# Attention on a 4 by 64 grid: keys kept column by column, 416 of 512 keys per query tile

## The chip, the cores and the metric

The kernel runs on one NeuronCore of a Trainium2 chip. The core has a matrix engine (TensorE, PE in the profile, with its weight loads listed as PEld), three engines that work on rows of data (VectorE or DVE, ScalarE or ACT, GpSimd or POOL), a queue engine that mostly starts transfers (SyncE or SP), and DMA engines that move data between DRAM and the on-chip memory SBUF. Results of TensorE land in eight PSUM banks. Each engine works through its own list of instructions in order, and waits on semaphores where it needs another engine's result. The metric is the device time of one execution in microseconds, as a median over runs.

## What is computed

Two layers over 256 latent tokens (a grid of 4 rows and 64 columns, width 2048) and 256 context tokens. The first layer has 16 heads of neighbourhood attention beside a state-space mixer (SSD, 8 groups of 4 heads); their outputs, gated, go through one output projection. The second is a short gated convolution. The change touches only the attention of the first layer:

```
rows = seq // GRID_W                       # 4; kh = min(8, rows) = 4, so every row sees all rows
col_start = clip(col - 8, 0, 48)           # a query column sees 16 key columns
mask      = (col' >= col_start) & (col' < col_start + 16)
s_lat = q . k * scale + rpb[h, row' - row + 7, clip(col' - col, -15, 15) + 15], masked to -inf
s_ctx = q . k_ctx * scale                  # all 256 context tokens, no bias
pr    = softmax([s_lat, s_ctx])            # 512 keys
out   = pr[:256] . v + pr[256:] . v_ctx
```

So each query has 4 x 16 latent keys and 256 context keys that count. Which latent keys these are depends on the query's column alone, not on its row. A block of queries of neighbouring columns needs only the keys of neighbouring columns.

## The kernel before

TensorE does nearly everything in three products: each float32 operand is split into a rounded part (type float32r) and the remainder, and H.H + H.L + L.H are added up in PSUM. `mm` (L195) issues every product, `turn` (L199) every transpose. Weights arrive from DRAM in tiles of 128 x 1024 (`raw`), are split by ACT (L420, rounded part) and DVE (L427, remainder) into one of three places `w`, and are used once.

The program works through one long sequence of weight products: the first 8 blocks of K, V, Q and B; then the gate, the time steps and the SSD inputs of the first quarter; then, for each further quarter, Q and K (`do_qk`), gate and V (`do_gv`), SSD inputs (`do_ssd`), with gate and V last in the last quarter; then the output projection in passes of 512 columns (the first pass does two of them), then the second layer. All other work is written as generators (`kq_gen`, `head_gen`, `group_gen`, `put_mix` and others) that hang between the weight products. A planner (class `Plan`) keeps a clock for each engine and prices each instruction as it is recorded. `pump` lets a generator go on when the planner's clocks say that its operands will be ready; `force`, called where the main sequence needs a result that is not recorded yet, records the pending steps in the order that the planner finds earliest, until that result is there. The order on each engine thus follows from the planner's prices: a change of one instruction can move many others. [...]

For one attention head (`head_gen`, L1033) the steps are: four transfers bring the head's bias rows from a staged copy in DRAM (`rpbs`, written at L929) into `bias` (L1039); DVE adds the column mask, 512 columns (L1044); for each of two query tiles of 128 queries (two grid rows), TensorE makes the scores against all 512 keys, 256 latent and 256 context (`score`, three products); DVE adds the bias and takes the row maximum (`top`, L1057), where the 256 context columns use a block of zeros that POOL has set (L932); ACT takes the exponential and its sum (L1062); DVE scales. TensorE transposes the weights in blocks of 128 keys, ACT and DVE split them into `PH` and `PL` (L1099, L1101), and V of the head into `VH` and `VL` (L1110, L1112). Then come 12 products: four key blocks, three products each, over all 256 queries. DVE multiplies with the gate (L1122), and `put_mix` (L939) writes the head's output to DRAM (L951) or, late in the program, splits it in place into a `mix` tile (L944, L946). K and Q of four heads at a time are normalised, transposed and split by `kq_gen` (L994, L996, L998, L1000); V goes from PSUM to `Vt` by `v_gen` (L1012).

An SSD group ends like this (`group_gen`, L1370): transfers bring decay rows from DRAM (L1391), ACT and DVE make the four decay matrices (the last product at L1420), TensorE multiplies them with the inputs `xtm`, DVE adds `yi` and gates with `sz` (L1439, L1442), ACT squares (L1444), DVE adds (L1449), TensorE sums over the channels against a column of ones, DVE and POOL make the inverse root (L1460, L1462), TensorE spreads it by two transposes of `r`, DVE scales (L1472), and `put_mix` hands two more `mix` tiles to the output projection. The output projection takes the 32 `mix` tiles in a fixed order: 0 to 11, 16 to 31, 12 to 15. Heads 12 to 15 are the last group of attention, 30 and 31 the last SSD group.

## Time and profile before

| | |
|---|---|
| median of three runs | 1762.85 us (1761.52 to 1763.02) |
| profiled execution | 1760.31 us, span 1758.5 us |
| mean granted TensorE clock | 0.999 |
| busy: PE, PEld, DVE, ACT, POOL | 1736.7, 1463.1, 1223.6, 773.4, 31.6 us |
| moved by DMA | 377.66 MB |
| DMA packets | 202536, of which 32384 under 512 B |

How to read the rows: a group has the line of the program, the engine, the operation, `written<-read` by the program's names, the shape and the count; after the bar its busy time and the mean length of one in ns; after the second bar the idle time of the engine just ahead of it and what ended it. A row of the timeline or the chain has its start and its length in us from the start of the span. Lengths of products include the pipeline's latency, so products overlap in the list, and the pace of a stream is read from the distance of the starts. A plain float32 product appears as two records.

### The profile page before, as it was taken

Reading aid. Unit: us, or ns where it says so; the run is one execution under the profiler, and the core shown is the slowest. Engines: PE = TensorE matmul, PEld = TensorE weight load, DVE = VectorE, ACT = ScalarE, POOL = GpSimd, SP = SyncE. Lnnn points to the kernel's source line nnn. Section 1 sums busy time; section 2 is a strip of 40 time slices with the busy share of each in tenths; the row PEclk is TensorE's granted clock in tenths of the full one; section 3 lists DMA queues with packets and bytes.
Section 4 is the critical chain, followed back from the end, with each engine's and each line's share of the span. In section 5 each row is a group of like instructions: output and inputs, shape, how many; then the busy total and the mean of one; then the engine's idle time right before and its main releaser. Section 6 shows DMA issues by size and latency. Waiting matters only on the chain.

```text
span 1758.5 us, 25025 instructions
## 1 busy us (share of the span) xinstructions
PE 1736.7 (99%) x9451; PEld 1463.1 (83%) x9451; DVE 1223.6 (70%) x1978; ACT 773.4 (44%) x1330; POOL 31.6 (2%) x28
## 2 busy tenths in 40 slices
PE   6999999999999999999999999999999999999998
PEld 4777988889888889888888898888888888888887
DVE  5666887878685878686877787787668555555554
ACT  5333544445242436343435343564446444444442
POOL 0000100001000000000000000000000000000000
PEclk9999999999999999999999999999999999999999
DMA  9987644686756767656776557768767666666563
GB/s 362 342 307 258 209 143 138 183 246 191 234 165 195 219 205 227 210 175 210 220 213 193 166 185 255 246 221 284 274 222 228 195 188 192 192 191 188 190 208 121
DMA packets 202536, 377.66 MB, mean 215 GB/s; under 512 B 32384, under 2 KB 69040, under 8 KB 202416
## 3 DMA queue, kind: packets, MB, share of 16 engines
q1 hardware_dynamic: 195152, 369.49, 65.5%
q10 hardware_dynamic: 7264, 6.58, 1.1%
q8 instruction: 74, 1.21, 0.3%
q14 instruction: 46, 0.38, 0.1%
HBM read 370.62 MB, written 6.71 MB: 215 GB/s over the span
## 4 chain that ended last, share of the span: by engine, by line
PE 94%; DMA 2%; DVE 2%; issue 1%; ACT 0%; POOL 0%; SPq 0%; ACTq 0%; DVEq 0%; POOLq 0%
PE bank L195 91%; PE bank L199 3%; DMA tmp<-dram_csr 1%; DVE w L427 1%; DMA raw<-in_ada 0%; DMA tmp<-dram_exr 0%; DMA raw<-in_adaT 0%; DVE tmp L1235 0%; ACT w L420 0%; POOL statk L572 0%; DVE mix L1562 0%; SPq L583 0%; DVE raw L823 0%; DVE tmp L603 0%; DVE Vt L1012 0%
## 5 line engine op out<-in xcount | busy, mean ns | idle before, releaser
L420 ACT CAST w<-raw 128x1024 fp32r<-128x1024 f32 x343 | 359.5, 1049 | 530.4 <-PE bank L195 447.7
L427 DVE TENSOR_TENSOR w<-raw,w 128x1024 fp32r<-128x1024 f32 x343 | 416.6, 1217 | 231.4 <-ACT w L420 230.1
L195 PE MATMUL bank<-hH,w 128*128 128x256 f32 (+1 forms) x2064 | 488.0, 324 | 1.2 <-DVE w L427 1.1
L195 PE MATMUL bank<-w,hH 128*128 128x512 f32 x1280 | 407.4, 396 | 2.7 <-ACT hH L757 2.5
L195 PEld LDWEIGHTS bank<-hH,w 128*128 128x128 f32 x2064 | 344.7, 188 | 34.2 <-DVE w L427 2.1
L195 PE MATMUL bank<-hL,w 128*128 128x256 f32 (+1 forms) x1040 | 334.3, 321 | 0.0
L195 PEld LDWEIGHTS bank<-w,hH 128*128 128x128 f32 x1280 | 237.7, 189 | 54.4 <-issue 4.0
L195 PE MATMUL bank<-w,hL 128*128 128x512 f32 x640 | 249.9, 391 | 0.1
L195 PEld LDWEIGHTS bank<-hL,w 128*128 128x128 f32 x1040 | 196.3, 189 | 14.9
L195 PE MATMUL bank<-w,h 128*128 128x512 f32 x768 | 179.7, 390 | 0.0
L823 DVE CUSTOM_DVE_ANT_0 raw<-raw,csb 128x1024 f32<-128x1024 f32 x128 | 155.4, 1219 | 26.2 <-DMA raw<-in_adaT 24.0
L195 PEld LDWEIGHTS bank<-w,h 128*128 128x128 f32 x768 | 143.6, 188 | 29.6
L195 PEld LDWEIGHTS bank<-w,hL 128*128 128x128 f32 x640 | 120.5, 188 | 25.4 <-DVE hL L763 0.6
L195 PE MATMUL bank<-w,mix 128*128 128x512 f32 x588 | 138.3, 391 | 0.9 <-DVE w L427 0.9
L195 PEld LDWEIGHTS bank<-w,mix 128*128 128x128 f32 x588 | 109.5, 188 | 24.0 <-DVE w L427 1.3
L1235 DVE SCALAR_TENSOR_TENSOR tmp<-bank,cwh,tmp 128x508 f32<-128x508 f32 (+1 forms) x96 | 71.0, 744 | 1.8
L195 PE MATMUL bank<-KL,h 128*128 128x512 f32 x264 | 63.8, 389 | 0.0
L427 DVE TENSOR_TENSOR KL<-raw,KL 128x1024 fp32r<-128x1024 f32 x32 | 39.1, 1223 | 33.1 <-ACT KL L420 33.1
L427 DVE TENSOR_TENSOR wL<-raw,wH 128x1024 fp32r<-128x1024 f32 x31 | 37.9, 1224 | 33.5 <-ACT wH L420 33.4
L427 DVE TENSOR_TENSOR QL<-raw,QT 128x1024 fp32r<-128x1024 f32 x32 | 39.2, 1224 | 29.8 <-ACT QT L420 29.8
L195 PEld LDWEIGHTS bank<-KL,h 128*128 128x128 f32 x264 | 49.5, 188 | 10.2
L195 PE MATMUL bank<-QT,h 128*128 128x512 f32 x168 | 56.2, 391 | 0.0
(291 smaller groups left out, 1984.7 us busy)
## 6 DMA issues: line engine op xcount, KB each, us to landing
raw<-in_w_in SPq DMA_DIRECT2D x196, 512.0 KB, 3.9
raw<-in_adaT SPq DMA_DIRECT2D x128, 512.0 KB, 4.8
raw<-in_sc_in SPq DMA_DIRECT2D x128, 512.0 KB, 3.8
raw<-in_w_out SPq DMA_DIRECT2D x64, 512.0 KB, 5.0
raw<-in_ada SPq DMA_DIRECT2D x34, 512.0 KB, 6.9
raw<-in_sc_out SPq DMA_DIRECT2D x32, 512.0 KB, 4.1
PT<-in_ada SPq DMA_DIRECT2D x16, 512.0 KB, 6.9
raw<-in_w SPq DMA_DIRECT2D x16, 512.0 KB, 6.1
```

The source lines that it names most:

```text
L195: E(T.matmul(o, l, r, start=start, stop=stop, skip_group_check=True))
L199: E(T.transpose(o, i, ident if k == 128 else ident[:k, :k]))
L420: E(S.copy(H, v))
L427: E(V.tensor_tensor(out=Lo, in0=v, in1=H.bitcast(F32), op=ALU.subtract))
L823: E(V.tensor_tensor_reduce(out=raw, in0=raw, in1=csb, scale=1.0, scalar=0.0, op0=ALU.mult, op1=ALU.add, accum_out=gp[:, h, m:m + 1]))
L1235: E(V.scalar_tensor_tensor(out=do, in0=di, scalar=cwh[:, 32 * k + ch:32 * k + ch + 1], in1=do, op0=ALU.mult, op1=ALU.add))
```

## The change

Latent keys, queries and values are put in column order (column first, the four rows inside it), and each query tile is now a block of 32 grid columns rather than two grid rows. Query tile 0 holds columns 0 to 31 and needs key columns 0 to 39, tile 1 holds columns 32 to 63 and needs key columns 24 to 63: 160 of the 256 latent keys. The 512 keys stand in the order key columns 0 to 31, context, key columns 32 to 63, so each tile's keys are one run of 416: positions 0 to 415 for tile 0, 96 to 511 for tile 1.

- Scores, bias, maximum, exponential and scaling take 416 columns. DVE clears the 96 columns left (`top`).
- The products with the values take the two context blocks for all 256 queries, and each of the two latent blocks (32 key columns) for the 160 queries that see it (`BLOCKS`).
- The bias comes as a table made on the host, 672 columns a head, in one transfer; the staged copy and POOL's zeros go. The mask is added in three pieces.
- K and Q are written in column order by strided writes; K's latent tiles and all of Q's remainders take two instructions each (`kq_gen`).
- V is put in column order by a way through DRAM: four transfers out on ACT's queue and one in on SP's, for each group of four heads (`turn_v`).
- The gate multiplication reads PSUM with a stride to bring the output back to row order.

```diff
+    vd = drt([256, 512], "vd")
-    rpbs = drt([16, 64, 320], "rpbs")
-    E(DMA.dma_start(rpbs, bass.AP(tensor=rpb.tensor, offset=76, ap=[[465, 16], [0, 64], [1, 320]])))
-    for b_ in bias:
-        E(G.memset(b_[:, 2, :], 0.0))
...
+    def columns(ap, t):
+        return ap.rearrange("p h (c r) -> p h r c", r=4)[:, :, 2 * t:2 * t + 2, :]
+
+    def turn_v(a):
+        for t in range(2):
+            for r in range(2):
+                yield W_("AQ", Vt[:, t, :])
+                E(DMA2.dma_start(vd.rearrange("(c r) n -> c r n", r=4)[:, 2 * t + r, :], Vt[64 * r:64 * r + 64, t, :]))
+        yield W_("SP", vd)
+        E(DMA.dma_start(Vt[:, 0:2, :], vd.rearrange("(t p) n -> p t n", p=128)))
+        got.add(("V", a))
...
# kq_gen, K (t < 2: latent)
-                E(S.copy(dst[:, :, o], four(pt)))
-                E(V.tensor_tensor(out=low[:, :, o], in0=four(pt), in1=dst[:, :, o].bitcast(F32), op=ALU.subtract))
+                for dh_, _, i in places_:
+                    E(S.copy(dh_, i))
+                yield W_("DVE", dst)
+                for dh_, dl_, i in places_:
+                    E(V.tensor_tensor(out=dl_, in0=i, in1=dh_.bitcast(F32), op=ALU.subtract))
...
# v_gen
-        got.add(("V", a))
+        yield from turn_v(a)
...
# head_gen
+    BLOCKS = ((1, 2, slice(0, 256)), (2, 3, slice(0, 256)), (0, 0, slice(0, 160)), (3, 1, slice(96, 256)))
-        for r in range(4):
-            E(DMA.dma_start(bt[64 * (r % 2):64 * (r % 2) + 64, r // 2, :].rearrange("p (a b) -> p a b", a=4),
...
+        E(DMA.dma_start(bf, rpb[hd]))
-        E(V.tensor_tensor(out=bv, in0=bv, in1=mask.unsqueeze(1).to_broadcast([128, 8, 64]), op=ALU.add))
+        for o_, m_ in ((0, mask[:, 0:32]), (304, mid), (544, mask[:, 32:64])):
+            n_ = m_.shape[-1]
+            bv = bf[:, o_:o_ + 4 * n_].rearrange("p (c r) -> p c r", r=4)
+            E(V.tensor_tensor(out=bv, in0=bv, in1=m_.unsqueeze(2).to_broadcast([128, n_, 4]), op=ALU.add))
+        span = lambda qt: slice(96 * qt, 96 * qt + 416)
-            mm(ps, QT[:, h, o], KT[:, h, :], True, False)
+            mm(ps[:, :416], QT[:, h, o], KT[:, h, k_], True, False)
...
+            E(V.memset(sp[:, 0:96] if qt else sp[:, 416:512], 0.0))
-            E(S.activation(sp, sp, AF.Exp, bias=s4[:, 2 + qt:3 + qt], scale=1.0, accum_out=s4[:, 4 + qt:5 + qt]))
+            E(S.activation(sc, sc, AF.Exp, bias=s4[:, 2 + qt:3 + qt], scale=1.0, accum_out=s4[:, 4 + qt:5 + qt]))
...
-        for kt in range(4):
-            mm(po[:, :256], VH[:, kt], PH[:, kt, :], kt == 0, False)
-            mm(po[:, :256], VH[:, kt], PL[:, kt, :], False, False)
-            mm(po[:, :256], VL[:, kt], PH[:, kt, :], False, kt == 3)
+        for i, (kt, vt, q_) in enumerate(BLOCKS):
+            mm(po[:, q_], VH[:, vt], PH[:, kt, q_], i == 0, False)
+            mm(po[:, q_], VH[:, vt], PL[:, kt, q_], False, False)
+            mm(po[:, q_], VL[:, vt], PH[:, kt, q_], False, i == 3)
...
+    spawn(urgent, turn_v(0))
     spawn(urgent, kq_gen("K", 0, parK, 4, statk, KT, KL, False), 4)
```

## The prediction

> **What bounds the kernel now.** I read the page first (busy shares, then the chain that ended last), then the waits of PE.

> ```profile
> PE 1736.7 (99%) x9451; PEld 1463.1 (83%) x9451; DVE 1223.6 (70%) x1978; ACT 773.4 (44%) x1330; POOL 31.6 (2%) x28
> ...
> PE 94%; DMA 2%; DVE 2%; issue 1%; ACT 0%; POOL 0%; SPq 0%; ACTq 0%; DVEq 0%; POOLq 0%
> ```

> ```profile
> PE bank L195 <- DMA raw<-in_ada: 10.8, 1, 10.8
> ...
> PE bank L195 <- DVE w L427: 2.0, 3, 0.9
> ```

> TensorE bounds it: it is busy 99% of the span, 94% of the chain is its own work, and its largest wait, 10.8 us, is the first load. So two things count: how much shorter TensorE's stream gets, and whether the changed order leaves it waiting in a place where it does not wait today. Busy DVE and ACT time matters only through the second.

> **What one product costs.** The first row is from the chain (start, length, count); then the grouped forms, and one head's twelve products with the values from the timeline (start, length).

> ```profile
> 1671.73 82.32 PE bank L195 x363
> ```

> ```profile
> L195 PE MATMUL bank<-KT,QT 128*128 128x512 f32 x32 | 13.1, 408 | 0.0
> ```

> ```profile
> L195 PE MATMUL bank<-PH,VH 128*128 128x256 f32 x64 | 17.9, 279 | 0.0
> ```

> ```profile
> 1168.51 0.28 PE L195 MATMUL bank<-PH,VH 128*128 128x256 f32 x1
> ...
> 1169.90 0.86 PE L195 MATMUL bank<-w,mix 128*128 128x512 f32 x3
> ```

> The mean lengths include the pipeline's latency; what a stream pays is the distance between starts. A 512-column product costs 82.32/363 = 0.2268 us. A 256-column one costs (1169.90 - 1168.51)/12 = 0.1158 us. The slope is 0.111/256 = 0.434 ns a column.

> **Part 1, scores.** Three products per query tile, 2 tiles, 16 heads: 96 products (three groups of 32 such as KT,QT) go from 512 to 416 columns, between two widths that lie on this line. 96 x 96 x 0.434 ns = 4.0 us less, all on the bounding engine.

> **Part 2, products with the values.** 192 products (three groups of 64); two blocks of four, so 96 products, go from 256 to 160 columns. On the same line each would cost 0.1158 - 0.0417 = 0.074 us. But each product also loads 128 weight columns, and the trace shows narrow products that do not get cheaper (starts and counts, then weight loads by width, mean ns second):

> ```profile
> 256.46 0.58 PE L195 MATMUL bank<-half,half 128*128 128x32 f32 x4
> ...
> 256.88 0.48 PE L195 MATMUL bank<-hH,w 128*128 128x512 f32 x1
> ```

> ```profile
> L195 PEld LDWEIGHTS bank<-PH,VH 128*128 128x128 f32 x64 | 12.0, 188 | 0.6
> ...
> L195 PEld LDWEIGHTS bank<-tmp,xtm 128*64 128x64 f32 x128 | 6.8, 136 | 2.0 <-issue 1.2 <-DMA raw<-in_w_out 0.4
> ```

> ```profile
> L195 PE MATMUL bank<-tmp,Btmt 128*128 128x512 f32 x32 | 15.0, 592 | 0.0
> ```

> Four records that stream 32 or 64 columns over 128 weight columns still take 0.42/4 = 0.105 us each, and a weight load grows by (188 - 136)/64 = 0.81 ns per weight column, 104 ns for 128. So weight loading, which overlaps the product before it, holds the pace near 0.105 to 0.112 us however few columns stream. I take 0.112 (these are plain fp32, the new products are fp32r): 96 x 0.004 = 0.4 us gained. Low end: the line goes on to 0.074, 4.0 us gained. High end: no fp32r product under 256 columns is in the trace; if such a one ran like plain fp32 (16 products, two records each, 15.0/16 = 0.94 us per 512 columns) it would take 0.293 us, 96 x 0.177 = 17 us lost.

> [...]

> **Part 3, the other engines.**

> ```profile
> L1057 DVE CUSTOM_DVE_ANT_0 tmp<-bank,bias 128x512 f32<-128x512 f32 x16 | 11.0, 686 | 2.5 <-PE bank L195 2.5
> ...
> L1122 DVE TENSOR_TENSOR half<-bank,gt 128x256 f32<-128x256 f32 x16 | 6.7, 421 | 11.9 <-PE bank L195 11.8
> ```

> ```profile
> L1062 ACT ACTIVATE tmp<-tmp,s 128x512 f32<-128x512 f32 x32 | 23.1, 722 | 27.8 <-DVE s L1060 27.8
> ```

> ```profile
> L951 ACTq DMA_DIRECT2D dram_mixd<-half x24: 326/326/454, 272.8 to 992.1; - x24
> ```

> ```profile
> L1039 SPq DMA_DIRECT2D bias<-dram_rpbs x64: 573/614/2243, 223.6 to 1139.2; - x64
> ```

> ```profile
> csb<-dram_crow SPq DMA_DIRECT2D x6, 512.0 KB, 5.8
> dram_mixd<-half ACTq DMA_DIRECT2D x24, 128.0 KB, 3.1
> ```

> DVE, at (686 - 421)/256 = 1.04 ns a column with about 0.15 us fixed: 32 row maxima lose 0.1 us each (-3.2 us); 32 memsets of 96 columns (0.1 to 0.25 us, taken at 0.1: +3.2); 16 mask additions of 512 columns become three of 128, 64 and 128 (0.28 + 0.22 + 0.28 against 0.69: +1.5); 16 of the low halves of K and Q split in two (0.15 each: +2.4). About +4 us in 1224. ACT: 32 exponentials lose 0.08 us (-2.6), 8 split casts of K gain 0.15 to 0.2 (+1.4), 16 new DMA issues of 0.33 us (+5.2): about +4 in 773. SP issues 16 bias transfers in place of 64 of 0.61 us, 4 reads of V more, and the one staging copy goes: about 30 us of issue less. I cost all this at nothing: DVE and ACT idle 30% and 56%; were the cover gone, the 8 us are the most it costs.

> V goes to DRAM and back for each group of four heads: four writes (0.33 us of ACT each, 3.1 us to land), one read (0.6 to issue, 5.8 to land), about 11 us later than today. Heads wait for it holding no PSUM bank, and the projections go on. Where it is tightest, at the last group, the changed program's order puts 78 products of 512 columns (17.7 us) between the last product with the values and the first that reads any of the last four heads' outputs; I cost it at nothing; were V over 17 us later than the planner allows for, TensorE would wait for the excess.

> **Part 4, what the planner moves.** The weight products come in the same sequence, but everything hung between them is placed anew. On PE's list, the end of the last SSD group stands so before (top) and after (below); `mix_9736` and `mix_9829` are the same block:

> ```
> 4937 L195 Matmult bank_87<-tmp_73,xtm 64x128 x4        (then 18 products)
> 4944 L195 Matmult bank_82<-const,half_81 128x1 x2      (then 15)
> 4950 L199 Matmult bank_85<-const,r_1_1634 128x128 x2   (then 24)
> 4959 L195 Matmult bank_86<-w_95,mix_9736 128x512 x3
>
> 4956 L195 Matmult bank_82<-tmp_69,xtm 64x128 x4
> 4957 L195 Matmult bank_85<-const,half_74 128x1 x2
> 4958 L199 Matmult bank_89<-const,r_1_1631 128x128 x2
> 4959 L195 Matmult bank_87<-w_95,mix_9829 128x512 x3
> ```

> Each of the four needs a result that DVE, ACT or POOL make from the one before. Before, 57 products (12.9 us) cover those steps; after, none. The steps as they ran before:

> ```profile
> 1170.71 0.98 SPq L1391 DMA_DIRECT2D tmp<-dram_csr  x2
> ...
> 1186.41 0.42 DVE L1420 TENSOR_TENSOR tmp<-tmp 128x256 f32<-128x256 f32 x1
> ...
> 1187.81 1.05 ACT L420 CAST w<-raw 128x1024 fp32r<-128x1024 f32 x1 [1.66 <-PE bank L195]
> 1188.38 1.09 PE L195 MATMUL bank<-tmp,xtm 128*64 128x128 f32 x16
> ...
> 1188.89 1.23 DVE L427 TENSOR_TENSOR w<-raw,w 128x1024 fp32r<-128x1024 f32 x1 [0.93 <-ACT w L420]
> ...
> 1190.03 0.42 DVE L1439 TENSOR_TENSOR half<-bank,yi 128x256 f32<-128x256 f32 x1
> ...
> 1192.19 0.42 DVE L1449 TENSOR_TENSOR half<-half,half 128x256 f32<-128x256 f32 x1 [0.48 <-ACT half L1444]
> ...
> 1193.62 0.50 PE L195 MATMUL bank<-const,half 128*128 128x1 f32 x4
> ...
> 1194.81 0.15 DVE L1460 TENSOR_SCALAR r<-bank 128x2 f32<-128x2 f32 x1
> ...
> 1195.04 0.70 POOL L1462 TENSOR_TENSOR r<-r,const 128x2 f32<-128x2 f32 x1 [51.01 <-DVE r L1460]
> ...
> 1197.53 0.38 PE L199 MATMUL bank<-const,r 128*128 128x128 f32 x2
> ...
> 1197.94 0.87 DVE L1472 SCALAR_TENSOR_TENSOR half<-half,small,bank 128x256 f32<-128x256 f32 x2 [0.62 <-PE bank L199]
> 1198.72 0.70 ACT L944 CAST mix<-half 128x256 fp32r<-128x256 f32 x2
> ...
> 1200.00 0.76 DVE L946 TENSOR_TENSOR mix<-half,mix 128x256 fp32r<-128x256 f32 x2
> ```

> Back to back: gate and square, 1190.03 to 1192.61 = 2.58; sums 0.50; 0.15; 0.70; transpose 0.38; one of two scalings 0.44; one cast 0.35; one low half 0.38: 5.5 us, and some eight handovers of 0.08 (1194.96 to 1195.04): 6.1. One thing lengthens it: on DVE's new list a low half of weights stands ahead of the gating, and its cast waits for the last product before the four, so gating starts 1.05 + 1.22 = 2.3 us after that product, not 1.1 us with the end of `xtm`: +1.0. Of this PE works 0.88 itself, which the sum has already. A stall of 6.2 us. The step ahead of it is tight too: from the issue of the last decay rows (1170.71) to the last product on DVE (1186.83) took 16.1 us with waits for other work; after, 54 products (12.2 us) stand between them: 0 to 3.9 us late, I take 1. Together 7 us. Low end 4 (no low half in the way, short handovers), high end 11 (the full 3.9, and DVE or ACT busy otherwise).

> **Sum.** -4.0 - 0.4 + 7 = +2.6, with 0.4 for small waits elsewhere +3.0 us. Against the profiled execution's own 1760.31 us this is 1763.3; that execution is 2.5 us below the median of the runs, 1762.85, so I give 1766 for a median. 0.2% (3.5 us) is about what a measurement of this kernel can tell from no change.

> **Rivals.**
> (B) The narrow products go on along the line, 0.074 us: -4.0 - 4.0 + 7.4 (stall and small waits) = -0.6, 1762. For it: no narrow fp32r product is in the trace. Against: the 0.105 us of the 32- and 64-column records.
> (C) Faster: the tail is covered. PE's queue only has to arrive there later than the steps finish, or other waits go that I can't see; with a stall of 0 to 3 us the time is 1758.5 to 1761.5. For it: before, PE waits there for nothing. Against: the list has no product in between, and PE runs in order. It decides at a stall under 4.4 us, the gain of parts 1 and 2.
> (D) Much slower: fp32r under 256 columns runs at the plain fp32 pace, +17 in place of -0.4: 1762.85 - 4.0 + 17 + 7.4 = 1783. From 0.117 us a product on, nothing of part 2's gain is left, and the stall decides alone. For it: nothing but that every fp32r product in the trace has 256 or 512 columns. Against: the weight load explains a flat cost without it.

> **Chances.** Forecast (flat cost, stall 4 to 11: 0 to +7 us, 1763 to 1770): 0.61; B 0.12; C 0.14; D 0.13. The forecast's half above +3.5 us, D and some of B with a long stall: slower 0.52. C's part below -3.5, B with a short stall and unseen waits that go: faster 0.17. The rest, 0.31, within 0.2%. Range: from C's lower end with some of B, 1757.5, up past the forecast's 1770 by the 4 us of DVE that I cost at nothing, 1774; D is left out.

> **What would show it.** Scores 0.186 us from start to start; 160-column products 0.105 to 0.115; a gap on PE of 4 to 8 us between `xtm` and the sums, followed by two of about 1 us, at about 1190; PE's busy time about 4 us lower elsewhere. Wrong if that gap is absent, if 160-column products are at 0.074 or over 0.15, or if PE waits for Vt or bias.

## The result: 1.0% slower, and the profile after

The changed kernel takes 1779.65 us (median of five runs, 1777.32 to 1781.63). The kernel before takes 1762.85 in the same session (median of five runs, 1758.83 to 1766.31). The ratio is 1.0097, 95% interval 1.0079 to 1.0116: slower by 16.8 us, where the prediction had 1766 and a range up to 1774. The profiled execution took 1779.64 us with a span of 1777.8, against 1758.5 before: 19.3 us more.

First the page of the changed kernel: busy time, and the chain by engine.

```profile
PE 1741.2 (98%) x9451; PEld 1467.0 (83%) x9451; DVE 1227.7 (69%) x2058; ACT 777.6 (44%) x1338; POOL 32.1 (2%) x26
...
PE 89%; DMA 5%; DVE 4%; issue 1%; ACT 1%; POOL 0%; SPq 0%; ACTq 0%; DVEq 0%
```

TensorE's busy time is up by 4.5 us although it streams less, and its share of the chain fell from 94% to 89%: something else now ends the time in places. The waits of PE (us in total, times, longest) say where.

```profile
PE bank L195 <- DVE half L1477: 4.9, 2, 4.1
PE bank L195 <- DVE w L427: 4.4, 7, 1.5
PE bank L199 <- DVE KL L1014: 3.1, 1, 3.1
...
PE bank L199 <- DVE tmp L985: 1.3, 1, 1.3
PE bank L199 <- POOL r L1490: 1.1, 1, 1.1
PE bank L195 <- ACT mix L940: 1.0, 1, 1.0
```

Of these only `DVE w L427` was in the list before, with 2.0 us. The others are new: the end of the last SSD group (`half L1477`, `r L1490`, `mix L940`), and K of the first stage (`KL L1014`, `tmp L985`).

The products themselves run as forecast. One tile's scores and one head's products with the values, from the timeline (start, length):

```profile
1161.67 0.24 PE L195 MATMUL bank<-PH,VH 128*128 128x160 f32 x1
1161.75 0.28 PE L195 MATMUL bank<-PL,VH 128*128 128x160 f32 x1
...
1162.19 0.28 PE L195 MATMUL bank<-PH,VL 128*128 128x160 f32 x1
...
1166.41 0.35 PE L195 MATMUL bank<-KT,QT 128*128 128x416 f32 x1
1166.60 0.35 PE L195 MATMUL bank<-KL,QT 128*128 128x416 f32 x1
```

Scores start 0.19 us apart. The 160-column products start (1162.19 - 1161.75)/4 = 0.11 us apart, the first one 0.08: over all 96 of them the mean is 0.105, against 0.117 for those of 256 columns. So the stream itself became 4.0 + 96 x 0.0118 = 5.1 us shorter.

Then the tail, TensorE's timeline (start, length, idle before and what ended it) and, in windows of 1 us, the granted clock (the third number from the right; the busy times of the engines stand to its left):

```profile
1210.85 1.39 PE L195 MATMUL bank<-tmp,xtm 128*64 128x128 f32 x16
1216.36 1.01 PE L195 MATMUL bank<-const,half 128*128 128x1 f32 x4 [4.12 <-DVE half L1477]
1218.47 0.69 PE L199 MATMUL bank<-const,r 128*128 128x128 f32 x2 [1.10 <-POOL r L1490]
1220.17 8.01 PE L195 MATMUL bank<-w,mix 128*128 128x512 f32 x24 [1.01 <-ACT mix L940]
```

```profile
1214.00:1215.00 1.00, 0.00 (x0) 0.00 (x0) 0.93 (x4) 0.37 (x1) 0.00 (x0) 0.90 1.00 305
1215.00:1216.00 1.00, 0.00 (x0) 0.00 (x0) 0.52 (x2) 0.47 (x2) 0.00 (x0) 0.50 0.85 332
...
1224.00:1225.00 1.00, 1.00 (x3) 0.74 (x3) 0.00 (x0) 0.00 (x0) 0.00 (x0) 0.50 0.66 258
1225.00:1226.00 1.00, 1.00 (x6) 0.80 (x5) 0.00 (x0) 0.52 (x1) 0.00 (x0) 0.98 0.08 33
```

Three idle times of 4.12, 1.10 and 1.01 us stand where part 4 put them. But while TensorE idles its granted clock falls to 0.50 and stays there until 1225, so 24 products take 8.01 us where 24 x 0.2268 = 5.4 would do.

To place all that is lost I add up, over the whole trace, the distances between the starts of successive products less the time that their columns stream (0.434 ns each), where this excess is over 0.15 us; products on a slow clock are in it, the slower stream of plain float32 products (0.94 us per 512 columns by the prediction's row) is not. In us:

| | total | 200 to 500 | 1100 to 1200 | 1200 to 1300 | elsewhere |
|---|---|---|---|---|---|
| before | 17.3 | 1.8 | 1.1 | 0.0 | 14.4 |
| after | 41.0 | 9.5 | 6.2 | 10.4 | 14.9 |

23.7 us more lost, less 5.1 gained, is 18.6 of the 19.3 us. Three places hold it: the first stage (7.7), the start of the output projection (5.1), the tail (10.4).

### The profile page after: what moved, and what is told of

It reads as the page before. It is cut to its first block, busy times and chain, and to the rows that moved or that the text cites. A ratio compares the mean times of both kernels' runs of the same rounds, so it can differ in the third digit from the quotient of the medians.

```text
span 1777.8 us, 25099 instructions
## 1 busy us (share of the span) xinstructions
PE 1741.2 (98%) x9451; PEld 1467.0 (83%) x9451; DVE 1227.7 (69%) x2058; ACT 777.6 (44%) x1338; POOL 32.1 (2%) x26
## 4 chain that ended last, share of the span: by engine, by line
PE 89%; DMA 5%; DVE 4%; issue 1%; ACT 1%; POOL 0%; SPq 0%; ACTq 0%; DVEq 0%
PE bank L195 86%; PE bank L199 4%; DMA raw<-in_adaT 3%; DVE w L427 1%; DVE raw L823 1%; DMA raw<-in_ada 0%; DMA csb<-dram_crow 0%; DMA tmp<-dram_csr 0%; DMA bias<-in_rpb 0%; ACT w L420 0%; POOL statk L572 0%; DVE tmp L1443 0%; DVE mix L1591 0%; DVE tmp L1263 0%; DVE half L1467 0%
## 5 line engine op out<-in xcount | busy, mean ns | idle before, releaser
L420 ACT CAST w<-raw 128x1024 fp32r<-128x1024 f32 x343 | 359.5, 1049 | 558.1 <-PE bank L195 478.6
L427 DVE TENSOR_TENSOR w<-raw,w 128x1024 fp32r<-128x1024 f32 x343 | 415.9, 1217 | 220.2 <-ACT w L420 214.7
L195 PE MATMUL bank<-hH,w 128*128 128x256 f32 (+1 forms) x2064 | 489.3, 325 | 1.6 <-DVE w L427 1.6
L195 PE MATMUL bank<-w,hH 128*128 128x512 f32 x1280 | 405.8, 395 | 2.7 <-ACT hH L757 2.5
L195 PEld LDWEIGHTS bank<-hH,w 128*128 128x128 f32 x2064 | 345.2, 188 | 35.5 <-DVE w L427 3.0
L195 PE MATMUL bank<-hL,w 128*128 128x256 f32 (+1 forms) x1040 | 334.8, 322 | 0.0
L195 PEld LDWEIGHTS bank<-w,hH 128*128 128x128 f32 x1280 | 237.2, 188 | 54.7 <-issue 3.9
L195 PE MATMUL bank<-w,hL 128*128 128x512 f32 x640 | 249.3, 390 | 0.1
L195 PEld LDWEIGHTS bank<-hL,w 128*128 128x128 f32 x1040 | 196.7, 189 | 14.3
L823 DVE CUSTOM_DVE_ANT_0 raw<-raw,csb 128x1024 f32<-128x1024 f32 x128 | 156.0, 1221 | 59.9 <-DMA raw<-in_adaT 58.2
L195 PE MATMUL bank<-w,h 128*128 128x512 f32 x768 | 179.5, 390 | 0.0
L195 PEld LDWEIGHTS bank<-w,h 128*128 128x128 f32 x768 | 143.6, 188 | 29.5
L195 PE MATMUL bank<-w,mix 128*128 128x512 f32 x588 | 143.2, 400 | 4.8 <-DVE w L427 2.8
L195 PEld LDWEIGHTS bank<-w,hL 128*128 128x128 f32 x640 | 120.1, 188 | 25.1 <-DVE hL L763 0.6
L195 PEld LDWEIGHTS bank<-w,mix 128*128 128x128 f32 x588 | 112.0, 193 | 30.0 <-DVE w L427 4.0
L195 PE MATMUL bank<-KL,h 128*128 128x512 f32 x264 | 63.8, 389 | 0.0
L427 DVE TENSOR_TENSOR KL<-raw,KL 128x1024 fp32r<-128x1024 f32 x32 | 39.2, 1225 | 34.5 <-ACT KL L420 34.5
L427 DVE TENSOR_TENSOR QL<-raw,QT 128x1024 fp32r<-128x1024 f32 x32 | 39.2, 1224 | 33.3 <-ACT QT L420 33.2
L427 DVE TENSOR_TENSOR wL<-raw,wH 128x1024 fp32r<-128x1024 f32 x31 | 38.0, 1224 | 32.4 <-ACT wH L420 32.3
L195 PEld LDWEIGHTS bank<-KL,h 128*128 128x128 f32 x264 | 49.5, 188 | 10.2
L195 PE MATMUL bank<-QT,h 128*128 128x512 f32 x168 | 56.2, 391 | 0.0
## 6 DMA issues: line engine op xcount, KB each, us to landing
raw<-in_w_in SPq DMA_DIRECT2D x196, 512.0 KB, 3.9
raw<-in_adaT SPq DMA_DIRECT2D x128, 512.0 KB, 4.6
raw<-in_sc_in SPq DMA_DIRECT2D x128, 512.0 KB, 3.7
raw<-in_w_out SPq DMA_DIRECT2D x64, 512.0 KB, 4.9
raw<-in_ada SPq DMA_DIRECT2D x34, 512.0 KB, 7.0
raw<-in_sc_out SPq DMA_DIRECT2D x32, 512.0 KB, 3.8
PT<-in_ada SPq DMA_DIRECT2D x16, 512.0 KB, 7.1
raw<-in_w SPq DMA_DIRECT2D x16, 512.0 KB, 6.3
```

Of the source, the lines that this page charges most:

```text
L195: E(T.matmul(o, l, r, start=start, stop=stop, skip_group_check=True))
L420: E(S.copy(H, v))
L427: E(V.tensor_tensor(out=Lo, in0=v, in1=H.bitcast(F32), op=ALU.subtract))
L823: E(V.tensor_tensor_reduce(out=raw, in0=raw, in1=csb, scale=1.0, scalar=0.0, op0=ALU.mult, op1=ALU.add, accum_out=gp[:, h, m:m + 1]))
```

## The experiments

The table gives for each run the median, the ratio to the kernel before with its interval, and the lost time by the same count. The runs stand below it with their edits, by question. Three of them have the same order of instructions (after, wide, v_priced) and lose 41.0, 40.8 and 42.1 us, 9.5 to 10.7 in the first stage and 16.6 to 18.4 in the last column, so a difference of 1 to 2 us in this count is noise.

| run | us | ratio | lost | 200 to 500 | 1100 to 1300 |
|---|---|---|---|---|---|
| after | 1779.65 | 1.0097 [1.0079, 1.0116] | 41.0 | 9.5 | 16.6 |
| tail_last | 1772.84 | 1.0057 [1.0041, 1.0074] | 32.4 | 9.2 | 8.1 |
| tail_fill | 1777.94 | 1.0082 [1.0069, 1.0095] | 33.3 | 10.8 | 7.3 |
| before_held | 1772.00 | 1.0053 [1.0037, 1.0069] | 27.2 | 1.8 | 11.0 |
| wide | 1784.36 | 1.0121 [1.0108, 1.0135] | 40.8 | 10.3 | 16.6 |
| v_later | 1775.41 | 1.0069 [1.0049, 1.0089] | 37.2 | 5.3 | 18.4 |
| v_direct | 1757.13 | 0.9957 [0.9944, 0.9970] | 17.6 | 0.6 | 2.8 |
| gem_late | 1779.20 | 1.0082 [1.0055, 1.0110] | 38.4 | 9.3 | 7.8 |
| all3 | 1768.25 | 1.0023 [1.0008, 1.0037] | 28.1 | 7.3 | 1.0 |
| v_priced | 1778.40 | 1.0083 [1.0067, 1.0099] | 42.1 | 10.7 | 18.4 |
| before_trip | 1765.27 | 1.0009 [0.9999, 1.0020] | 21.5 | 2.8 | 4.8 |
| v_perm | 2262.31 | 1.2824 [1.2800, 1.2848] | | | |
| v_later_last | 1766.54 | 1.0013 [1.0002, 1.0025] | 26.2 | 7.3 | 5.3 |
| told_true | 1784.66 | 1.0118 [1.0100, 1.0135] | 46.5 | 9.2 | 15.4 |
| told_wide_later_last | 1765.94 | 1.0011 [0.9999, 1.0023] | 29.2 | 7.2 | 8.2 |
| untold_all | 1779.50 | 1.0090 [1.0077, 1.0104] | 41.4 | 9.1 | 8.0 |
| vg_untold | 1780.89 | 1.0098 [1.0086, 1.0111] | 39.7 | 7.9 | 9.3 |
| vg_later_last | 1762.90 | 0.9998 [0.9986, 1.0009] | 21.1 | 4.1 | 1.3 |

### Does the shorter stream reach the end? (wide)

```
-            mm(ps[:, :416], QT[:, h, o], KT[:, h, k_], True, False)      (and the other two)
+            mm(ps, QT[:, h, o], KT[:, h, :], True, False)
-            mm(po[:, q_], VH[:, vt], PH[:, kt, q_], i == 0, False)       (and the other two)
+            mm(po[:, 0:256], VH[:, vt], PH[:, kt, 0:256], i == 0, False)
```

> The changed kernel in the same order of instructions, but the 96 score products stream 512 columns again and the 96 narrow products with the values 256, the columns added being unused or zero. By the distances of starts in the two traces this costs 96 x 0.0417 + 96 x 0.0114 = 4.0 + 1.1 us. Theory (TensorE is the bound, so each ns of its stream passes to the end): 5.1 us more than the changed kernel, about 1785. Rival 1 (the shorter products only lengthen waits that DVE and ACT set): 0 to 2 us more. Rival 2 (the products of 416 or 160 columns cost the stream something that their starts don't show): 0 or less.

The time is 4.7 us above the changed kernel's, 4.6 by the spans. The intervals of the ratios overlap by a hair (1.0108 and 1.0116), but every run of wide (1783.41 to 1785.08) is above every run of the changed kernel, and the lost time is the same in a kernel whose stream is 5.1 us longer. The theory holds, and both rivals fall: what parts 1 and 2 save reaches the end.

### What does the tail cost? (tail_last, before_held, tail_fill)

```
-    order = list(range(0, 6)) + list(range(8, 16)) + [6, 7]
+    order = list(range(0, 6)) + list(range(8, 15)) + [6, 7, 15]
```

> The changed kernel with the two blocks of the last SSD group put at the end of the sequence of weight products (order 0 to 5, 8 to 14, 6, 7, 15), so that 40-odd other products stand on TensorE between the steps at the end of that group. In the trace of the changed kernel the idle time of TensorE at these steps sums to about 7.2 us (1214 to 1220), and the granted clock behind it is 0.50 from 1216 to 1224 us. Theory (the uncovered tail costs the idle time and, through the clock, as much again as half of it): 10 to 11 us less than the changed kernel, about 1769, and no stretch with a clock under 0.9 between 1200 and 1240. Rival 1 (only the idle time counts, the low clock would come anyway): 7 us less, 1772.5. Rival 2 (the idle time only moves elsewhere, since what DVE and ACT have to do there is what holds the end): under 3 us less.

By the medians it gained 6.8 us, which is what rival 1 said (7), by the spans 7.8, under the theory's 10 to 11. The place itself decides between the two: there the products are 10.3 us earlier than in the changed kernel and the clock stays at 1.00, as the theory has it. Behind it 2.4 us are given back in a new wait at 1223 us, where mix blocks come late (`PE bank L195 <- ACT mix L940: 1.4`).

```
+        yield when(lambda: (s, gi) != (3, 1) or let[0])      # kernel before; let[0] is set at the 14th block of weights
         yield W_("PE", Ds[3], nb=1)
         py = bank()
```

> The kernel before, unchanged but for the end of the last SSD group (its xtm products and all behind them), which is held back until the last weight products that don't need it are out; TensorE's list there is then the same as the changed kernel's, with no product between the four steps. Theory (the uncovered tail costs idle time and clock, whatever else the change did): 7 us of idle time, 0.5 of the clock for some 8 us behind it, and 10 to 11 us more than the kernel before, about 1773. Rival 1 (no throttle): 7 us more, 1770. Rival 2 (the tail is dear only with the changed kernel's DVE and ACT work around it): under 4 us more.

The kernel before, with nothing of the change in it, loses 0.53% [0.37, 0.69], 9.3 us, and 9.8 by the spans. Its timeline there, and the clock at the start and end of its low stretch:

```profile
1202.36 1.09 PE L195 MATMUL bank<-tmp,xtm 128*64 128x128 f32 x16
1207.33 0.61 PE L195 MATMUL bank<-const,half 128*128 128x1 f32 x4 [3.87 <-DVE half L1450]
1209.95 0.69 PE L199 MATMUL bank<-const,r 128*128 128x128 f32 x2 [2.02 <-POOL r L1463]
1211.65 13.65 PE L195 MATMUL bank<-w,mix 128*128 128x512 f32 x51 [1.01 <-ACT mix L944]
```

```profile
1208.00:1209.00 1.00, 0.00 (x0) 0.00 (x0) 0.96 (x2) 0.00 (x0) 0.72 (x1) 0.86 0.87 272
...
1215.00:1216.00 1.00, 1.00 (x5) 0.82 (x4) 0.00 (x0) 0.00 (x0) 0.00 (x0) 0.72 0.00 0
```

These are the same three idle places (6.9 us in all), and in the windows between the two shown the clock is 0.50, as in the changed kernel. The uncovered tail by itself costs 9 to 10 us.

```
+            T.matmul(b, QT[:, 0, 0:128], KT[:, 0, :], start=True, stop=True, ...)    # 18, 4 and 4 times, into a free bank
```

> The changed kernel with 26 extra products of 512 columns (18 after the xtm products, 4 after the sums, 4 after the transposes of the last SSD group; their results are not used), so that TensorE works where it idled, and nothing else is moved. 18 of them last 4.1 us, 4 of them 0.9 us. Theory (the idle time throttles the clock, and the products behind it pay): the granted clock stays at 1.0 from 1214 to 1226 and the time falls by 3 to 4 us against the changed kernel, to about 1776, although TensorE has 26 products more. Rival 1 (the low clock has another cause than the idle time): no change within 1.5 us, or up to 2 us more, and the clock shows the same dip.

TensorE's idle time is filled, the clock stays up (the third number from the right below is 1.00 through the stretch that had 0.50), and at the place the products are 2.9 us earlier than in the changed kernel, with 26 products more. Over the whole kernel 1.7 us are left of it, 0.7 by the spans (this profile is already 2.2 us later than the changed kernel's ahead of the place), and the intervals overlap. The effect at the place is shown; what it is worth at the end is not.

```profile
1214.00:1216.00 2.00, 2.00 (x13) 1.56 (x10) 2.00 (x4) 0.17 (x1) 0.00 (x0) 1.00 1.05 386
1216.00:1224.00 8.00, 7.86 (x36) 5.71 (x36) 4.93 (x12) 1.64 (x4) 0.70 (x1) 1.00 0.91 294
```

So of the 10.4 us of the tail about 7 are the idle time that part 4 worked out, and about 3 are the slow clock.

### Where do the other 13 us come from? (v_later, gem_late, all3)

```
-    spawn(urgent, turn_v(0))
     spawn(urgent, kq_gen("K", 0, parK, 4, statk, KT, KL, False), 4)
     spawn(urgent, kq_gen("Q", 0, psQ, 2, statq, QT, QL, True), 2)
+    spawn(urgent, turn_v(0))
```

> The changed kernel with the first turn of V through DRAM spawned behind the generators of K and Q in place of ahead of them (one line moved). In the trace of the changed kernel the products are 6.3 us later than before by 550 us, and TensorE waits 3.1 us at 241 us for a low half of K (DVE KL L1014), whose chain of squares on ACT ended at 211.8 us in place of 205.6. Theory (V's four issues and what is placed with them delay K): that wait goes, the products are at most 2 us later than before by 550 us, and the time is 4 to 5 us less than the changed kernel's, about 1775; the end of the last SSD group stays uncovered (7 us and a low clock). Rival (the dearer forms of K and Q on DVE and ACT, about 2.5 us each for one group of heads, keep K late wherever V stands): the wait stays within 1 us of 3.1, and the time within 1.5 us.

4.2 us less. The wait for `KL` is gone: TensorE's waits between 195 and 550 us are now these two, against `DVE KL L1014` 3.1, `DVE tmp L985` 1.3 and two smaller ones in the changed kernel. What was lost from 200 to 500 us falls from 9.5 to 5.3.

```profile
PE bank L195 <- DVE tmp L1448: 2.0, 1, 2.0
PE bank L195 <- DVE w L427: 0.9, 1, 0.9
```

The theory holds: V's turn, put ahead of K and Q on the list of urgent work, made K late. The 3.5 us by which this order still loses more than the kernel before (5.3 for 1.8) hold these two waits and a slow clock behind the first (see the last section); v_direct, without V's way, loses 0.6 there, and what makes the first of them was not tried.

At the start of the output projection the changed kernel shows TensorE waiting for the halves of weights, and once DVE blocked ahead of them by a product for the modulation whose load is late (two views: PE's timeline, then three lines of DVE's).

```profile
1120.48 3.11 PE L195 MATMUL bank<-w,mix 128*128 128x512 f32 x13
1124.15 2.83 PE L195 MATMUL bank<-w,mix 128*128 128x512 f32 x11 [0.56 <-DVE w L427]
1127.95 0.50 PE L195 MATMUL bank<-w,mix 128*128 128x512 f32 x1 [0.96 <-ACT w L420]
1129.21 6.00 PE L195 MATMUL bank<-w,mix 128*128 128x512 f32 x18 [0.76 <-DVE w L427]
...
1148.93 2.33 PE L195 MATMUL bank<-w,mix 128*128 128x512 f32 x9 [1.49 <-DVE w L427]
...
1126.33 1.28 DVE L1033 COPY Vt<-bank 128x512 f32<-128x512 f32 x2
1127.93 1.23 DVE L427 TENSOR_TENSOR w<-raw,w 128x1024 fp32r<-128x1024 f32 x1
...
1146.51 1.22 DVE L823 CUSTOM_DVE_ANT_0 raw<-raw,csb 128x1024 f32<-128x1024 f32 x1 [5.10 <-DMA raw<-in_adaT]
```

The late load explains the wait of 1.49 us at 1148.93, whose low half DVE makes right behind that product. The three waits before it (0.56, 0.96 and 0.76 us) stand behind other work in the queues of DVE and ACT: splits of `mix` blocks (L1590, L1591) and, ahead of the half for the one at 1129.21, V's copies (L1033); whether DVE's own earlier wait for such a load, 3.26 us to 1118.89, is behind them too is not shown. The last two of them also brought a slow clock from 1129.48 to 1132.88 (see the last section). The next run moves the modulation's products alone.

```
                     yield when(lambda: ("gem", m, h) in RAW)
+                    yield when(lambda: q != 1 or plan.t["PE"] >= plan.ready((RAW["gem", m, h][0],)) + 4000.0)
```

> The changed kernel with each product of the second modulation block on DVE (L823, which reads the loads of adaT) placed at least 4 us behind the time at which the planner expects its load; the new list also has products between the steps at the end of the last SSD group. In the trace of the changed kernel DVE waits 58.2 us in 41 places for these loads (24.0 in 27 before), and TensorE idles about 5 us at 1119 to 1150 us behind low halves of weights that stand behind such a wait. Theory (DVE's own queue is blocked by loads that come later than planned): DVE's waits for adaT fall under 25 us, TensorE's idle time at 1119 to 1150 us under 1.5 us, and with the tail covered the time is 12 to 14 us less than the changed kernel's, 1766 to 1768. Rival (the loads that hold the weights' buffers longer make the weights later): TensorE's waits for w L427 stay at 4 us or grow, and only the tail's 7 to 10 us are gained, or less: 1770 to 1773.

A miss. DVE's waits for these loads fell only to 28.9 us, and at the same place the two waits below stand, in its waits between 1115 and 1150 us: a load that is over 4 us later than planned still blocks DVE, and TensorE waits 3.8 us behind it. The covered tail was won (nothing lost from 1200 to 1300), and new waits elsewhere (4.9 us at 600 to 700) took it back.

```profile
DVE raw L824 <- DMA raw<-in_adaT: 4.3, 1, 4.3
...
PE bank L195 <- DVE w L427: 3.8, 1, 3.8
```

> The three edits together: V's first turn behind K and Q, the products of the second modulation block 4 us later, the last SSD blocks at the end of the sequence. Theory (the three losses are in different places and add up): 4.5 + 4 + 9 = 17 us less than the changed kernel, about 1762, level with the kernel before. Rival (the gains overlap, or the new order loses elsewhere): 1767 or more.

Its edits are v_later's, gem_late's and tail_last's. 11.4 us gained, not 17. The last column falls to 1.0, so the tail and the start of the output projection are clean; 3.5 us at 600 to 700, 2.8 at 900 to 1000 and 7.3 from 200 to 500 (5.3 in v_later) are this order's losses. Every new order tried here had its own.

### V's way through DRAM: the transfers, or the order? (v_direct, v_priced, before_trip)

v_direct leaves the way out of program and plan; v_priced leaves the transfers out and books their times with the planner. In both the heads take V's rows in the order of the tokens: what is left out is the putting of V in column order.

```
-                E(DMA2.dma_start(vd...[:, 2 * t + r, :], Vt[64 * r:64 * r + 64, t, :]))
+                plan.priced("ACT", Vt[64 * r:64 * r + 64, t, :], vd...[:, 2 * t + r, :])     (v_priced; v_direct has no line)
```

> The changed kernel without V's way through DRAM at all: the 16 writes and 4 reads are left out and the heads take V's rows in the order of the tokens, so the attention's values are not the reference's. Its list has products again between the steps at the end of the last SSD group. Theory (V's way costs nothing by its transfers, only by where it puts K's chain and by the planner's new order): late products by 550 us fall from 6.3 to at most 2 us, the tail's 10 us go, nothing else does: about 1765. Rival (heads wait for V, so the transfers themselves cost): products are also 2 us or more earlier than that between 600 and 1100 us, and the time is under 1761.

1757.13 us: the change without V's way is 0.43% faster than the kernel before [0.30, 0.56], and lost time is back at 17.6 us. What is left of PE's waits above 2 us is the first load and two short ones:

```profile
PE bank L195 <- DMA raw<-in_ada: 10.8, 1, 10.8
PE bank L195 <- ACT hH L757: 2.5, 2, 1.4
PE bank L195 <- DVE w L427: 2.2, 1, 2.2
```

Theory or rival, the gain alone does not say. The next run does.

> The changed kernel with the planner told of V's way through DRAM as before, so that every engine has the changed kernel's order of instructions to the last one, but with the 20 transfers themselves (16 writes, 4 reads) left out; the heads then take V's rows in the order of the tokens, so the attention's values are not the reference's. The kernel with neither transfers nor their prices in the plan was 22 us faster than the changed one. Theory (the new order of work costs those 22 us, and the transfers nothing): within 3 us of the changed kernel, 1777 to 1780, with the waits for KL at 240 us, for low halves of weights at 1119 to 1150 us and the uncovered tail all there. Rival (the transfers cost: their issues on ACT, their traffic against the loads, the heads that wait for V): 1757 to 1768.

Every engine has the changed kernel's order, no transfer of V is made, and the time is the changed kernel's, with all of its waits (line numbers are 24 higher in this kernel):

```profile
PE bank L219 <- DVE w L451: 5.2, 5, 2.8
PE bank L219 <- DVE half L1501: 4.9, 2, 4.1
PE bank L223 <- DVE KL L1038: 3.1, 1, 3.1
```

So, once they are planned for, the 20 transfers cost nothing that can be measured here (1778.40 us without them, 1779.65 with). The order does.

```
+        (turn_v added to the kernel before, at the same places, with vd[128 * t + 64 * r:128 * t + 64 * r + 64, :])
```

> The kernel before with V's way through DRAM alone added: the same 16 writes and 4 reads at the same places of the program, but in the order of the tokens both ways, so nothing else changes. In its list the steps at the end of the last SSD group have products between them. Theory (V's way, through K's late chain in the first stage and what the planner moves, costs some 6 us by 550 us and some 5 us at the start of the output projection, whatever the widths of the attention's products): 6 to 12 us more than the kernel before, 1769 to 1775. Rival 1 (V's way is hidden where the rest of the kernel is as before, and it was the whole change that made the order bad): within 3 us of the kernel before. Rival 2 (only the tail counts): within 3 us too, as the tail is covered here.

Rival 1: +0.09% [-0.01, 0.20], 4.2 us more lost, half of it in one wait at 1121 us (3.1, where the kernel before has 1.1), most of the rest in the clock of 0.50 behind that wait (1125.17 to 1128.58). In the kernel before the planner finds room for the same transfers. So V's way alone does not give the bad order; it takes V's way together with the rest of the change.

### Can an order with V's way in it keep the gain? (the other runs)

untold_all has v_direct's order on TensorE and DVE, with the transfers issued and not booked. vg_untold also projects V ahead of the gate in the last group.

```
-                E(DMA2.dma_start(vd..., Vt...))
+                DMA2.dma_start(vd..., Vt...)
```

> The changed kernel with all its transfers, but the planner not told of V's way: on TensorE and DVE the order is to the last instruction that of the kernel without V's way (v_direct, 1757), with the 20 transfers issued right behind V's copies. In the trace of v_direct the first use of V comes 78 us behind V in the first group, and 1 us behind it in the last (copies to 1121.7, cast of V at 1121.9). Theory (only the order counted; V late in the last group alone): as v_direct but for a wait of ACT for V of about 10 us at 1122, of which TensorE, which has the output projection's first products to do but whose weights are cast on ACT behind that wait, pays 3 to 10: 1760 to 1767. Rival 1 (V is late nowhere that matters): 1756 to 1759. Rival 2 (the order is good only with V's rows in place): 1770 or more.

> As untold_all, with V projected ahead of the gate in the last group of heads, so that the gate's products (768 of 256 columns, 22 us by the 0.1158 us of one... counted as 192 for one group) lie between V and its first use. All transfers are made, nothing is left out. Theory (V's way is then hidden everywhere and the narrow products' 5 us are kept): 1755 to 1760, faster than the kernel before. Rival (the new order of the last stage has its own gaps at the start of the output projection or at the end of the last SSD group): 1762 or more.

Both missed: 1779.5 and 1780.9. The first use of V comes soon behind V not in the last group alone, but in three of four, as PE's and ACT's waits in untold_all show:

```profile
PE bank L195 <- ACT VH L1140: 16.1, 3, 7.5
...
ACT VH L1140 <- DMA Vt<-dram_vd: 24.8, 3, 9.9
```

V's way kept ACT waiting up to 9.9 us, which something has to cover. I had looked at the first and the last group only. It must be in the plan; then it moves the plan.

```
             if ins[0].dtype == F32R:
-                return 9 + 0.434 * n, 190
+                return 9 + 0.434 * (self.as_ or n), 190     # as_ = 234 for the 160-column products: 111 ns
```

> The changed kernel with one number of the planner put right: 160-column products with the values priced at 111 ns, as they run, in place of 78. The order moves by some 140 instructions on TensorE, and 8 rows (of three products each, 5 us) then stand between the xtm products and the sums at the end of the last SSD group, with none between the sums and the transposes. Theory (the tail was uncovered by a hair, and the price decides it): idle time there of 2 to 3 us in place of 7.2, no low clock, 7 to 9 us less than the changed kernel, 1771 to 1773; the first stage unchanged. Rival (a better price moves other work into worse places): within 3 us of the changed kernel.

A miss: 5 us slower than the changed kernel. A truer price gave a worse order: 4.8 us are lost at 974 us and 6.4 at 1146. The tail loses 5.3 us in place of 10.4, with its two last steps still bare, so this one price did not make it alone.

> The changed kernel with V's first turn behind K and Q and the last SSD blocks at the end of the sequence. Alone these gave 4.2 and 6.8 us. Theory (two places, independent): 10 to 12 us less than the changed kernel, 1768 to 1770, with TensorE still waiting some 3 to 5 us at the start of the output projection. Rival (they overlap, as each time the work that is won early piles up at the start of the output projection): 1772 or more.

Its edits are v_later's and tail_last's. 13.1 us less than the changed kernel, 0.13% [0.02, 0.25] above the kernel before: the two gains add up, and somewhat more.

> The changed kernel with all its transfers, the planner told the old prices of the attention's products (512 and 256 columns) while the products are narrow, V's first turn behind K and Q, and the last SSD blocks at the end. Products stand between all the steps at the end of the last SSD group. Theory (with K early and the tail covered the change keeps its 5 us on TensorE but for what is lost at the start of the output projection, 3 to 5 us): 1762 to 1767. If that loss goes too: 1758, faster than the kernel before. Rival (other places lose as much): over 1769.

To the two edits of v_later_last it adds `as_` of 512 and 256 for the narrow products. 1765.94, in the range, and no better than v_later_last.

```
-                    qk + ssd_cols(a) + gv
+                    qk + ssd_cols(a) + gv[::-1]      (last group: V's weights and products ahead of the gate's)
```

> As v_later_last (1766.5), with V of the last group of heads projected ahead of its gate, so that the gate's 192 products of 256 columns (22 us) lie over V's way, which the planner is told of. Nothing is left out. Theory (what is lost at the start of the output projection comes from V's way pushing the last heads into it): TensorE's waits between 1100 and 1160 us fall from 3.7 us to under 1.5, and the time to 1762 to 1765, level with the kernel before. Rival (those waits are for low halves of weights that DVE makes late in any order): 1765 or more.

The edits of v_later_last and this one. 1762.9 us: 0.9998 of the kernel before [0.9986, 1.0009]. Three changes of order alone, all transfers made, win back the whole loss; from 1100 to 1300 us 1.3 us are lost in place of 16.6. It does not beat the kernel before. It loses 21.1 us for 17.3, above all from 200 to 500 (4.1 for 1.8) and in one wait of 2.8 us at 1099, and that eats most of the 5.1 us of shorter products. Whether a better order exists stays open. The version without V's way shows what it would be worth.

A way to have V's rows in order without moving V: load x and the context in the order of the columns of the grid, and let the products that need the tokens in order read their moving operand at a distance.

```
-            E(DMA.dma_start(xt[...], src[r0:r0 + 128, ...]))
+            E(DMA.dma_start(xt[...], src.rearrange("(r c) d -> c r d", r=4)[r0 // 4:r0 // 4 + 32, :, ...]))
-            mm(o, H[:, bb], actH[:, :n], f, False)          (and the others of mm_ws and of the step sizes)
+            mm(o, H[:, bb], actH[:, :n].rearrange("p (s c r) -> p s r c", c=64, r=4), f, False)
```

> The changed kernel with the rows of x and of the context loaded in the order of the columns of the grid, so that K, Q and V stand in that order without V's way through DRAM and without the scattered writes of K and Q; the products for the gate and the SSD parts read their moving operand with a distance of four elements in place of one, to have the tokens in order. Nothing is left out. Theory (a moving operand read at a distance of four elements streams at the same pace, and V's way was what cost the time): as the kernel without V's way, 1755 to 1759, below the kernel before. Rival (such a read is slower): 1152 products of 512 columns at 0.2268 us and 1920 of 256 at 0.1158 make 484 us of the span, so each per cent that they slow down costs 4.8 us; at 2% the kernel before is the faster one, at a tenth it is 1805.

2262 us. The rival, at its far end; see the last section.

## Why the prediction was wrong, step by step

**Right.** TensorE bounds it. Part 1: 0.19 us per score product, 4.0 us gained. Part 2: the cost is flat, not on the line: 0.105 for 0.117, a gain of 1.1 us where I took 0.4. The 0.105 us agrees with the 104 ns that the prediction works out for a load of 128 weight columns; that these loads set the pace is my estimate, which no run tried, and no row shows the 0.112 that I took. wide shows that the gain reaches the end. Rivals B and D fell with it, and C with the tail.

**Part 4, right in place, too small.** "Together 7 us": the idle time sums to 6.2 us and with slower small steps to about 7. What I left out is the clock: 4.12 us of idle time took it to 0.50, and the last section shows that less was enough elsewhere. The term measured 10.4 in the changed kernel and, by the same count, 9.9 in before_held. (A slip in its sum: gating 2.3 us behind the last product and not 1.1 us adds 1.2, not 1.0.)

**The step that failed** is the end of the sum, "with 0.4 for small waits elsewhere". It measured 12.8 us: 7.7 in the first stage and 5.1 at the start of the output projection, waits in both and a stretch of 3.4 us at half the clock, about 1.7 us lost each by my estimate. I compared the two lists at one place, the one where the four steps of the tail had lost their cover, and took the rest of the new order for as good as the old. The first stage needed the same look: v_later shows that V's turn, put ahead of K's chain there, cost some 4 us.

**Part 3** had its totals right (DVE 1227.7 for 1223.6, ACT 777.6 for 773.4, as the +4 and +4 said), by luck, and its cover wrong. The +4 of ACT held 5.2 us of DMA issues, which the profile does not count as busy. In their place stand writes in column order that cost more than I took: K's casts are 5.9 us longer in sum (I took 1.4), Q's scaled copies 4.0 (1.19 us each for 0.69; I took nothing), and on DVE the low halves of K and Q 9.6 (I took 2.4). Of the cover: "DVE and ACT idle 30% and 56%" is a mean over the span, and at 225 to 245 us and at 1120 to 1148 us the engines that TensorE waited for stood in their own queues. The sentence on V's way, "I cost it at nothing", was right for the transfers (v_priced, before_trip) and wrong for the plan: with V's way in the plan the kernel is 22 us slower than without (v_direct).

With the measured terms the sum is -4.0 - 1.1 + 10.4 + 12.8 + 0.5 elsewhere = 18.6, of 19.3 us between the spans. The upper end of the range, 1774, had 11 us for the tail and 4 for the cover of DVE, which is why it failed by 6.

Not settled: why the planner came to this order. V's way is needed for it (v_direct), and not enough (before_trip); one truer price made it worse (told_true).

## What to carry to other kernels

Where a planner or a list scheduler makes the order, split a change into its work and its new order, and measure them apart: keep the order and undo the work (wide, v_priced), or undo the work's place and keep the work (tail_last, v_later). Compare the two lists at every chain of small steps, not only at the worst one, and for each ask what stands between its steps. An idle time of TensorE of some 2 us or more (1.89 us by the count in the last section) is to be priced with the slow clock that can follow it; at the tail that cost about half as much again, 3 us on 7.

## What the runs showed of the hardware that I had not expected

```profile
242.00:243.00 1.00, 1.00 (x6) 0.74 (x4) 1.00 (x3) 0.80 (x2) 0.00 (x0) 0.51 0.94 340
...
245.00:246.00 1.00, 1.00 (x4) 0.48 (x3) 0.97 (x2) 0.99 (x3) 0.00 (x0) 0.79 0.05 13
...
1129.00:1130.00 1.00, 0.79 (x2) 0.63 (x3) 0.15 (x1) 1.00 (x2) 0.00 (x0) 0.74 0.38 128
...
1132.00:1133.00 1.00, 1.00 (x4) 0.76 (x4) 1.00 (x4) 0.59 (x2) 0.00 (x0) 0.56 0.85 223
```

Since the windows inside a stretch read 0.50 and those outside it 1.00, a mean gives the moment: from 242.02 to 245.42 and from 1129.48 to 1132.88, 3.40 us each. In before_held it is 1208.72 to 1215.56, 6.84 us, and in untold_all, behind a wait for V, 10.24 again:

```profile
754.00:755.00 1.00, 0.00 (x0) 0.00 (x0) 0.00 (x0) 0.00 (x0) 0.00 (x0) 0.93 0.18 63
...
765.00:766.00 1.00, 1.00 (x6) 0.83 (x5) 1.00 (x3) 0.38 (x1) 0.00 (x0) 0.95 0.89 286
```

All five are 1, 2 or 3 times 3.41 us (10.24/3 = 3.413), and the three falls in the changed kernel are 887.46 and 85.32 us apart, 260 and 25 times 3.413.

So the price of an idle time here depends on where it falls. Cut into windows of this grid, the nineteen profiles of this case show how (windows that run at full clock, from 150 us on): each of the 31 with 1.89 us or more without a product is followed by one at 0.50, none of those with 1.70 us or less is, and of the ten in between three are. In the changed kernel the windows with 2.76 and 2.58 us (from 238.60 and 1211.40) and one with 1.72 (from 1126.06) are, one with 1.49 (from 1146.54) is not. The idle time need not be in one piece: ahead of 1129.48 one product starts at 1127.95, between idle times of 0.96 and 0.76 us. Nor need it be as long as the 4.12 us of the tail: in v_later the wait of 2.0 us for `tmp L1448` was followed by a clock of 0.50 from 398.76 to 402.16.

```profile
398.00:399.00 1.00, 1.00 (x5) 0.85 (x5) 1.00 (x3) 0.87 (x3) 0.00 (x0) 0.88 0.04 12
...
402.00:403.00 1.00, 1.00 (x5) 0.77 (x5) 0.97 (x3) 0.28 (x1) 0.00 (x0) 0.92 0.76 201
```

In vg_later_last a longer one, 2.67 us at 1099, left the clock at 1.00: it lay across a border of the grid, 1.06 us in one window and 1.62 in the next.

**In v_perm a moving operand at a distance of four elements streamed at half the pace.** The 256-column products of one projection (start and length):

```profile
819.74 0.65 PE L195 MATMUL bank<-hH,w 128*128 128x256 f32 x2
820.21 0.41 PE L195 MATMUL bank<-hL,w 128*128 128x256 f32 x1
...
824.64 0.65 PE L195 MATMUL bank<-hH,w 128*128 128x256 f32 x2
```

Seven groups of three in 4.90 us are 0.233 us a product, against 0.1158 at a distance of one: a factor of two. Over the whole kernel TensorE is busy 2234.1 us for the changed kernel's 1741.2, 493 us more, which is nearly the whole difference between 2262 and 1757.
